# The first group's four x blocks begun together, feature by feature, and x fetched by two queues

## The chip, the cores and the metric

The kernel runs on one core of a Trainium2 chip. The metric is the device time in microseconds, 1324.78 as the median of three runs (1324.66 to 1325.58). One further execution was taken by the profiler; it took 1324.6 us, and its span, from the first to the last instruction, is 1322.9 us. TensorE (PE) multiplies, VectorE (DVE) and ScalarE (ACT) do the element-wise work, GpSimd (POOL) masks and starts transfers, SyncE (SP) starts the weight transfers.

## The reference

Two layers over 512 tokens of 1024 features: a Mamba-2 mixer and a ConvFFN, then differential attention and a second ConvFFN. Only the head of the Mamba-2 mixer is touched:

```python
zxbcdt = rms_norm(x, ln_g) @ in_w           # z 2048, x 2048, B 512, C 512, dt 32 columns
xbc = silu(causal_dwconv(xbc, conv_w, conv_b))
dt = softplus(dt + dt_bias); a = dt * (-exp(a_log))
y = ssd_chunked(xs * dt, a, B, C)           # 4 chunks of 128 tokens, 4 groups of 8 heads
y = (y + xs * d_skip) * silu(z)             # then a norm per group, and @ out_w
```

In `ssd_chunked` the running sums of `a` within a chunk give decays between tokens (a 128 x 128 matrix per head and chunk) and decays into and out of the chunk's state.

## The kernel before

**Products.** Every float32 product is made of three: an operand is split into a high part (ACT: `wh`, `xgh`) and the rest (DVE: `wl`, `xgl`), and `mm3` (L195) adds high by high, high by low and low by high. A block of the input projection is 128 output columns by 512 tokens in one PSUM bank: 8 features of 128 rows, 3 matmuls each, 24 in all (L196 to L198). The norm's factor per token, `rr`, is multiplied in when DVE takes the block out of PSUM.

**The start.** SP fetches x in four blocks of 128 tokens (`load_x`, L237): two, then the 32 dt columns (`dt_chunk`), then the first weight chunk (B of group 0, `in32`), then the other two. ACT's queue fetches the gain `st0` and the convolution's weights. TensorE runs seven placeholder products on the tile of ones (`busy`, L278), then turns each token block into features (`turn`, L287) in four auxiliary banks; a bank holds two features of two token blocks, that is of half the tokens. `split_x` (L292) takes a feature's half out as `xgh` and `xgl`, in the order `TURNS` = 0, 2, 4, 6, 1, 3, 5, 7. As the halves come, `dt_part` and `b0_part` (L298, L308) do dt and B's block in halves of 256 tokens, with small placeholder products between the first. The second half's `turn` needs the banks that the first half's splits release.

**Then** come, each as a whole block: C (`in36`), the four x blocks (`in16` to `in19`), and the first z block, `in0`. Weights come through `plan` in order of use: `chunk` (L187) asks for a chunk two ahead, SP fetches it into one of three raw buffers, ACT and DVE split it into one of three pairs. Each block goes to `conv_silu` (L610): DVE multiplies by `rr`, ACT starts the width-4 convolution, DVE adds three shifted terms, ACT applies SiLU.

**Decays.** dt is turned to tokens, softplus is a chain of some twenty small DVE operations (L645 to L664), then three matmuls `ps_dec` (L668) give the running sums, ACT their exponential, DVE copies, TensorE turns them (L687), and POOL writes them to DRAM (`cumd`) and reads them back spread over partitions (`fetch`, L706). POOL masks them and ACT takes 32 exponentials (`decays`). `scan` (L811) then goes through the four chunks, woven with the remaining z blocks.

**What sets the order.** A planner orders the instructions of each engine at compile time by priority, which follows the order of the program, and by its own estimate of when each is ready; on the chip each engine then goes through its list in that order. `pin` keeps an instruction in the program's order among the pinned ones of its engine; `tc.high_priority` moves a stretch ahead by an offset. Transfers are issued in order per queue.

Of the kernel before, what the change touches and what calls it, by code (L numbers as in the profile page):

```python
# [38 lines left out]
def trunk_kernel(ctx: ExitStack, tc, x, ssm_ln_g, ssm_in_w, ssm_conv_w, ssm_conv_b, ssm_dt_bias,  # L39
# [28 lines left out]
    plan.append(("dt", *w_cols(in_w, 0, KB, DI + CONV_DIM, NH)))  # L68

# [59 lines left out]
    WARM = (7, 64)  # L129
# [6 lines left out]
    def emit_chunk(pin=lambda i: i, later=None):  # L136
# [25 lines left out]
        else:  # L162
            def convert():
                pin(act.activation(wh[:, :n], raw[:, :n], AF.Copy))  # L164
                pin(dve.tensor_tensor(out=wl[:, :n], in0=raw[:, :n], in1=wh[:, :n].bitcast(F32), op=ALU.subtract))  # L165
# [7 lines left out]
    def dt_chunk():  # L173

        key, src, nk, ncol = plan[0]
        state["next"] = state["use"] = 1
        raw = wrp.tile([P, 1024], F32, tag="raw", name="wr_dt")
        rv = raw[:, :nk * ncol].rearrange("p (k c) -> p k c", k=nk)
        wv = w_dt.rearrange("p (k j c) -> p k j c", k=nk, j=2)
        sync.dma_start(rv, src)  # L180

        def convert():
            pin(act.activation(wv[:, :, 0, :], rv, AF.Copy))
            pin(dve.tensor_tensor(out=wv[:, :, 1, :], in0=rv, in1=wv[:, :, 0, :].bitcast(F32), op=ALU.subtract))
        return wv, convert
# [9 lines left out]
    def mm3(ps, wh, wl, xh, xl, start, stop):  # L195
        pe.matmul(ps, wh, xh, start=start, stop=False)  # L196
        pe.matmul(ps, wh, xl, start=False, stop=False)  # L197
        pe.matmul(ps, wl, xh, start=False, stop=stop)  # L198


# [30 lines left out]
    with tc.tile_pool(name="ph0", bufs=1) as p0:  # L231
# [4 lines left out]
        later = []  # L236
        load_x = lambda b: sync.dma_start(xt[b], x[0, b * P:(b + 1) * P, :])  # L237
# [60 lines left out]
        def dt_part(h, i):  # L298
            k, ts = TURNS[i], half[h]
            both = lambda: pin(pe.matmul(ps_dt[:2 * NH, ts], wdt[:, k].rearrange("p j c -> p (j c)"),  # L300
                                         xgh[k][:, ts], start=(i == 0), stop=(i == KB - 1)))
            if i < KB - 1:
                both()
            pin(pe.matmul(ps_dt[:NH, ts], wdt[:, k, 0, :], xgl[k][:, ts], start=False, stop=False))
            if i == KB - 1:
                both()

        def b0_part(h, i):  # L308
            k, ts = TURNS[i], half[h]
            pin(pe.matmul(ps_b0[:, ts], wb0[0][:, k, :], xgh[k][:, ts], start=i == 0, stop=False))  # L310
            pin(pe.matmul(ps_b0[:, ts], wb0[0][:, k, :], xgl[k][:, ts], start=False, stop=False))

        def b0_rest(h, i0=0, i1=KB):
            for i in range(i0, i1):
                k, ts = TURNS[i], half[h]
                pin(pe.matmul(ps_b0[:, ts], wb0[1][:, k, :], xgh[k][:, ts], start=False, stop=i == KB - 1))

        TURNS = (0, 2, 4, 6, 1, 3, 5, 7)
# [3 lines left out]
        ps_dt, ps_b0 = mm_bank("ps_dt"), mm_bank("ps_in32")  # L322
        wb0 = ready[0][1:]
        for b in range(2):
            for q in range(4):
                turn(0, b, q)
        for i in range(KB):
            if i == 1:
                convert_dt()
            split_x(0, TURNS[i])  # L330
        later.pop()()
        emit_chunk(pin, later)
        pv.append([view(aux_bank("xgt1_%d" % q)) for q in range(4)])
        for i in range(KB):
            dt_part(0, i)
            if i < 4:
                busy(1, WARM[1])
            elif i >= 6:
                turn(1, 2, i - 6)
        turn(1, 2, 2)  # L340
        turn(1, 2, 3)
        for i in range(KB):
            b0_part(0, i)
            if 1 <= i < 5:
                turn(1, 3, i - 1)
        b0_rest(0)
        for i in range(KB):
            split_x(1, TURNS[i])
        later.pop()()
        for i in range(KB):  # L350
            dt_part(1, i)
            b0_part(1, i)
        b0_rest(1)
        junk = [p0.tile([P, D], F32, name="sq%d" % i) for i in range(2)]
        for b in range(2):
            pin(act.activation(junk[0], xt[b], AF.Square, accum_out=rs[:, b:b + 1]))
            pin(dve.tensor_tensor_reduce(junk[1], xt[b + 2], xt[b + 2], 1.0, 0.0, ALU.mult, ALU.add,
                                         rs[:, b + 2:b + 3]))
        emit_chunk(pin)
        chunk("in32")  # L360
        ps = aux_bank("pst")
        pe.transpose(ps[:, :120], st1, ident[:120, :120])
        dve.tensor_copy(c1[:, :120], ps[:, :120])
# [22 lines left out]

    def rsqrt(v, pl, name, shape, n):

        m = pl.tile(shape, F32, tag="rs_m", name="rsm_" + name, bufs=2)
        t = pl.tile(shape, F32, tag="rs_t", name="rst_" + name, bufs=2)  # L390
        dve.tensor_scalar(out=m, in0=v, scalar1=1.0 / n, scalar2=EPS, op0=ALU.mult, op1=ALU.add)
        dve.tensor_scalar(out=v.bitcast(I32), in0=m.bitcast(I32), scalar1=1, scalar2=None,
                          op0=ALU.logical_shift_right)
        dve.tensor_scalar(out=v.bitcast(I32), in0=v.bitcast(I32), scalar1=-1, scalar2=0x5F3759DF,
                          op0=ALU.mult, op1=ALU.add)
        for _ in range(3):
            dve.tensor_tensor(out=t, in0=v, in1=v, op=ALU.mult)
            dve.scalar_tensor_tensor(out=t, in0=t, scalar=-0.5, in1=m, op0=ALU.mult, op1=ALU.mult)
            dve.scalar_tensor_tensor(out=v, in0=t, scalar=1.5, in1=v, op0=ALU.add, op1=ALU.mult)
# [26 lines left out]
    def along_tokens(r, name, step=2):  # L426

        ps = aux_bank("al_" + name)
        for b in range(NT):
            pe.transpose(ps[:, b * P:(b + 1) * P], r[:, step * b:step * b + 1].to_broadcast([P, P]), ident)  # L430
        return ps
# [984 lines left out]
```

## Time and profile before

| What | Value |
|---|---|
| Median of three runs | 1324.78 us (1324.66 to 1325.58) |
| Profiled execution | 1324.6 us |
| its span | 1322.9 us |
| TensorE busy | 1314.1 us, 99% |
| VectorE busy | 1026.0 us, 78% |
| ScalarE busy | 679.4 us, 51% |
| First whole block (C) begins | 20.94 us |
| First z block ends | 56.3 us |

An engine counts as busy while an instruction of its own runs; matmuls overlap each other, and their ends are modelled, so one matmul's length is read from the distance between starts. Lines such as L289 are those of the kernel. A row of the order of time has the start, the length, the engine (PEld is TensorE's weight load, SPq and ACTq are queues that start transfers), the line, the operation, its output and inputs, and in brackets the idle time just before it and what ended that. A count x8 means eight like instructions merged into one row.

### The profile page before, as it was taken

The page shows a single profiled execution, that of the slowest core. Times are in us where ns is not written, and L with a number is a line of the kernel's source. Part 1 is how long each engine was busy: PE and PEld are TensorE (multiplying, and loading weights), DVE is VectorE, ACT ScalarE, POOL GpSimd, SP SyncE. Part 2 cuts the span into 40 slices and gives each one's busy share as a digit, 9 for nine tenths or more (in the row PEclk, how much of TensorE's full clock was granted, in tenths as well). Part 3 has the DMA queues.
Part 4 walks back from the last instruction along what each step waited for, and adds up shares of the span by engine and source line. Part 5 has one row for each costly group of instructions (what it writes and reads, how often), then busy time and mean ns, then how long its engine had stood idle before and what let it go on. Part 6 is the DMA issues. An engine that isn't in the chain of part 4 may idle for free.

```text
span 1322.9 us, 17237 instructions
## 1 busy us (share of the span) xinstructions
PE 1314.1 (99%) x6441; PEld 1084.6 (82%) x6441; DVE 1026.0 (78%) x1740; ACT 679.4 (51%) x1148; POOL 59.4 (4%) x96
## 2 busy tenths in 40 slices
PE   9999999999999999999999999999999999999998
PEld 8778788888888888888888887777898888888887
DVE  6898977878868786878779645787778787778777
ACT  5665536336364443444345645776574443444343
POOL 5330300300000000000000000000000000000000
PEclk9999999999999999999999999999999999999999
DMA  7553432532317306320620333221236206320601
GB/s 208 156 152 96 152 97 79 167 96 66 109 50 239 96 0 206 105 73 1 205 82 1 117 103 88 71 80 57 64 95 209 80 1 222 96 65 0 213 27 64
DMA packets 166771, 135.09 MB, mean 102 GB/s; under 512 B 6044, under 2 KB 137824, under 8 KB 166688
## 3 DMA queue, kind: packets, MB, share of 16 engines
q1 hardware_dynamic: 161920, 121.75, 30.9%
q0 software_dynamic: 4496, 12.05, 3.0%
q8 instruction: 51, 0.84, 0.3%
q14 instruction: 32, 0.26, 0.1%
q10 hardware_dynamic: 272, 0.18, 0.0%
HBM read 131.72 MB, written 2.25 MB: 101 GB/s over the span
## 4 chain that ended last, share of the span: by engine, by line
PE 91%; DVE 5%; ACT 2%; DMA 1%; issue 1%; SPq 0%; DVEq 0%; ACTq 0%
PE ps_g L916 18%; PE ps_u L916 18%; PE ps_y L1061 7%; PE ps_x L1061 7%; PE ps_out L540 7%; PE ps_in L196 4%; PE ps_in L197 4%; PE ps_in L198 4%; PE ps_ao L540 3%; PE ps_k L1116 3%; PE ps_v L1116 3%; PE ps_q L1116 3%; PE ps_z L1061 2%; PE lg L1213 1%; PE po L1262 1%; DVE wl_in L165 1%
## 5 line engine op out<-in xcount | busy, mean ns | idle before, releaser
L916 PE MATMUL ps_g<-xgh,wl_g 128*128 128x512 f32 (+1 forms) x368 | 139.9, 380 | 0.0
L916 PE MATMUL ps_g<-xgl,wh_g 128*128 128x512 f32 (+1 forms) x368 | 139.9, 380 | 0.0
L916 PE MATMUL ps_g<-xgh,wh_g 128*128 128x512 f32 (+1 forms) x368 | 139.8, 380 | 0.0
L916 PE MATMUL ps_u<-xgh,wh_u 128*128 128x512 f32 (+1 forms) x368 | 139.3, 380 | 0.0
L916 PE MATMUL ps_u<-xgl,wh_u 128*128 128x512 f32 (+1 forms) x368 | 139.1, 380 | 0.0
L916 PE MATMUL ps_u<-xgh,wl_u 128*128 128x512 f32 (+1 forms) x368 | 137.6, 380 | 0.0
L196 PE MATMUL ps_in<-xgh,wh_in 128*128 128x512 f32 x312 | 125.5, 402 | 0.0
L197 PE MATMUL ps_in<-xgl,wh_in 128*128 128x512 f32 x312 | 123.8, 397 | 0.0
L198 PE MATMUL ps_in<-xgh,wl_in 128*128 128x512 f32 x312 | 122.3, 392 | 0.0
L989 ACT ACTIVATE wh_f<-dr 128x1024 fp32r<-128x1024 f32 (+1 forms) x72 | 71.3, 990 | 86.3 <-PE ps_y L1061 31.2
L990 DVE TENSOR_TENSOR wl_f<-dr,wh_f 128x1024 fp32r<-128x1024 f32 (+1 forms) x72 | 81.5, 1134 | 30.4 <-ACT wh_f L989 29.0
L165 DVE TENSOR_TENSOR wl_g<-wr_g,wh_g 128x1024 fp32r<-128x1024 f32 x44 | 53.8, 1224 | 51.9 <-ACT wh_g L164 51.9
L1006 ACT ACTIVATE hh<-f 128x256 fp32r<-128x256 f32 (+2 forms) x66 | 46.2, 700 | 77.6 <-DVE f L1018 74.2
L165 DVE TENSOR_TENSOR wl_u<-wr_u,wh_u 128x1024 fp32r<-128x1024 f32 x44 | 53.8, 1224 | 34.3 <-ACT wh_u L164 34.2
L916 PEld LDWEIGHTS ps_g<-xgh,wl_g 128*128 128x128 f32 x368 | 69.2, 188 | 13.4 <-DVE wl_g L165 0.2
L916 PEld LDWEIGHTS ps_g<-xgh,wh_g 128*128 128x128 f32 x368 | 69.2, 188 | 13.1
L916 PEld LDWEIGHTS ps_g<-xgl,wh_g 128*128 128x128 f32 x368 | 69.2, 188 | 13.1
L916 PEld LDWEIGHTS ps_u<-xgl,wh_u 128*128 128x128 f32 x368 | 69.2, 188 | 13.1
L916 PEld LDWEIGHTS ps_u<-xgh,wh_u 128*128 128x128 f32 x368 | 69.2, 188 | 13.1
L916 PEld LDWEIGHTS ps_u<-xgh,wl_u 128*128 128x128 f32 x368 | 68.2, 188 | 13.1
L1015 ACT ACTIVATE vg<-vg 128x512 f32<-128x512 f32 x44 | 27.9, 633 | 91.1 <-DVE vg L953 91.1
L953 DVE SCALAR_TENSOR_TENSOR vu<-ps_u,cf,vu 128x511 f32<-128x511 f32 x88 | 65.7, 747 | 9.6 <-ACT vu L951 8.6
(354 smaller groups left out, 3169.3 us busy)
## 6 DMA issues: line engine op xcount, KB each, us to landing
wr_g<-in_ffn_up_w_dram SPq DMA_DIRECT2D x44, 512.0 KB, 3.9
wr_u<-in_ffn_up_w_dram SPq DMA_DIRECT2D x44, 512.0 KB, 4.0
wr_in<-in_ssm_in_w_dram SPq DMA_DIRECT2D x40, 512.0 KB, 3.9
dr<-in_ffn_down_w_dram SPq DMA_DIRECT2D x16, 1024.0 KB, 9.4
m<-cumd POOLq DMA_DIRECT2D x16, 512.0 KB, 5.2
wr_out<-in_ssm_out_w_dram SPq DMA_DIRECT2D x16, 512.0 KB, 4.0
dr<-in_ffn_down_w_dram SPq DMA_DIRECT2D x8, 768.0 KB, 8.3
wr_k<-in_kv_w_dram SPq DMA_DIRECT2D x8, 512.0 KB, 3.8
```

Source lines behind the costliest of these rows:

```text
L165: pin(dve.tensor_tensor(out=wl[:, :n], in0=raw[:, :n], in1=wh[:, :n].bitcast(F32), op=ALU.subtract))
L196: pe.matmul(ps, wh, xh, start=start, stop=False)
L197: pe.matmul(ps, wh, xl, start=False, stop=False)
L198: pe.matmul(ps, wl, xh, start=False, stop=stop)
L540: m = pe.matmul(ps, x, w[:, k % 2, :], start=k == 0 and i == 0, stop=k == 3 and i == 2)
L916: pin(pe.matmul(ps[:, ts], a[:, k, :], x[k][:, ts], start=k == 0 and i == 0, stop=k == KB - 1 and i == 2))
L953: dve.scalar_tensor_tensor(out=v[:, s:], in0=ps[:, :T - s], scalar=col(2 - s), in1=v[:, s:], op0=ALU.mult, op1=ALU.add)
L989: act.activation(wh, src, AF.Copy)
L990: dve.tensor_tensor(out=wl, in0=src, in1=wh.bitcast(F32), op=ALU.subtract)
L1006: act.activation(fl(h[:, lo:hi, :]), fl(f[:, lo:hi, :]), AF.Copy)
L1061: pin(pe.matmul(bank[b], x, w_[:, q - a, :], start=start and q == 0 and i == 0, stop=end and q == a + n - 1 and i == 2, skip_group_check=T ...
L1116: m = pe.matmul(pss[b], x[k][:, ts], a[:, k - k0, :], start=k == 0 and i == 0, stop=k == KB - 1 and i == 2)
```

## The change

- **Transfers.** Blocks 0 and 1 are fetched in halves of 64 partitions, one by SP and one by ACT (`load_halves`). The x blocks' weights are fetched by feature instead of by block: one slice (`load_w`) has 128 rows of 512 columns, all four blocks' columns for one feature, into buffers of their own (`rawx`). SP's order is: half of block 0, slice 0, half of block 1, slice 1, block 2, slice 2, block 3, slices 3 to 7, dt's columns (`raw_dt`), then `plan`, which starts with B and C and has no dt and no x of group 0. The gain `st0` goes second in ACT's queue.
- **Start.** Instead of dt and B the halves feed the four x blocks, in the four main PSUM banks: `x_part(i, ts)` does feature `TURNS[i]` for all four blocks, 12 matmuls. Features 0 to 3 of the order go by halves, the fifth at full width for all blocks (`BY_BLOCK`), the last three block by block (`x_rest`). `split_w` splits a slice, and the splits of slices 0, 1 and 2 stand ahead of the features' splits. dt follows at full width in an auxiliary bank. One placeholder product stands in place of four.
- **Order behind it.** The root of the norm and the dt chain come earlier in the program, the chain at high priority. Then x0 to x3, B, C and the first z block, pinned; the decays' matmuls after C, and their transposes behind the first four features (12 matmuls) of the first z block (`turn_decays`). `fetch`, `params_a` and `turn_b` of group 0 come after that z block.

```diff
-    plan.append(("dt", *w_cols(in_w, 0, KB, DI + CONV_DIM, NH)))
...
-        for b in range(4):
-            plan.append(in_chunk(16 + 4 * g + b))
+        if g:
+            for b in range(4):
+                plan.append(in_chunk(16 + 4 * g + b))
...
-    WARM = (7, 64)
+    WARM = (7, 1)
+
+    BY_HALF, BY_BLOCK = 4, 5
...
-        load_x = lambda b: sync.dma_start(xt[b], x[0, b * P:(b + 1) * P, :])
-        load_x(0)
-        load_x(1)
-        wdt, convert_dt = dt_chunk()
-        emit_chunk(pin, later)
+        rawx = [p0.tile([P, 1024], F32, name="rawx%d" % i) for i in range(KB // 2)]
+        raw_dt = p0.tile([P, KB, NH], F32, name="raw_dt")
+        load_x = lambda b: pin(sync.dma_start(xt[b], x[0, b * P:(b + 1) * P, :]))
+        cols_of = lambda i: slice((i % 2) * 512, (i % 2 + 1) * 512)
+        load_w = lambda i: pin(sync.dma_start(rawx[i // 2][:, cols_of(i)],
+                                              in_w[TURNS[i] * P:(TURNS[i] + 1) * P, DI:DI + 512]))
+
+        def load_halves(b):
+
+            for q, ps in ((sync, slice(0, 64)), (act, slice(64, P))):
+                pin(q.dma_start(xt[b][ps], x[0, b * P + ps.start:b * P + ps.stop, :]))
+
+        load_halves(0)
+        pin(act.dma_start(st0, ssm_ln_g.rearrange("o (b p) -> (o b) p", p=P)))
+        load_w(0)
+        load_halves(1)
+        load_w(1)
         load_x(2)
+        load_w(2)
         load_x(3)
-        act.dma_start(st0, ssm_ln_g.rearrange("o (b p) -> (o b) p", p=P))
+        for i in range(3, KB):
+            load_w(i)
+        pin(sync.dma_start(raw_dt, in_w[:, DI + CONV_DIM:DI + CONV_DIM + NH].rearrange("(k p) c -> p k c", p=P)))
...
+        def split_w(i):
+            (h, l), r, cs = wx[i // 2], rawx[i // 2], cols_of(i)
+            pin(act.activation(h[:, cs], r[:, cs], AF.Copy))
+            pin(dve.tensor_tensor(out=l[:, cs], in0=r[:, cs], in1=h[:, cs].bitcast(F32), op=ALU.subtract))
+
+        def x_part(i, ts, blocks=range(4)):
+            (h, l), k = wx[i // 2], TURNS[i]
+            for j, (w, f) in enumerate(((h, xgh), (l, xgh), (h, xgl))):
+                for b in blocks:
+                    c = (i % 2) * 512 + b * P
+                    pin(pe.matmul(ps_x[b][:, ts], w[:, c:c + P], f[k][:, ts],
+                                  start=i == 0 and j == 0 and ts.start == 0, stop=i == KB - 1 and j == 2,
+                                  skip_group_check=True))
...
+        busy(WARM[1], 64)
+        for i in range(3):
+            side(i)
         for i in range(KB):
-            if i == 1:
-                convert_dt()
+            if i < 3:
+                split_w(i)
             split_x(0, TURNS[i])
-        later.pop()()
-        emit_chunk(pin, later)
+        split_w(3)
...
+        for i in range(3):
+            x_part(i, half[0])
+        for qs in ((0, 1), (2, 3)):
+            for b in (2, 3):
+                for q in qs:
+                    turn(1, b, q)
+            if qs[0] == 0:
+                x_part(3, half[0])
         for i in range(KB):
             split_x(1, TURNS[i])
-        later.pop()()
-        for i in range(KB):
-            dt_part(1, i)
-            b0_part(1, i)
-        b0_rest(1)
+            if i in (4, 6):
+                split_w(2 + i // 2)
...
+        for i in range(4):
+            x_part(i, half[1])
...
+        for i in range(BY_HALF, BY_BLOCK):
+            x_part(i, slice(0, T))
         emit_chunk(pin)
...
+        x_rest(0)
...
+                if g == 0:
+                    if b:
+                        x_rest(b)
+                    conv_silu(b, ps_x[b], xs[b])
+                    continue
...
+            if g == 0:
+                conv_block(16, "in32", bT, True)
+                conv_block(20, "in36", cT, True)
...
+                z = z_blocks(g, zs, (4, turn_decays))
+                next(z)
+                for c in cs:
+                    c.fetch()
+                params_a()
+                turn_b(g, bT, cs)
```

More of the change, by code (lines that the diff above doesn't have):

```diff
@@ L134, in trunk_kernel, with emit_chunk @@
     pin = tc.keep_in_program_order
[L136 removed]
+    def emit_chunk(pin=lambda i: i):
         i = state["next"]
@@ L296, in split_x, with side @@
                                          in1=xgh[m][:, half[h]].bitcast(F32), op0=ALU.mult, op1=ALU.subtract))
[L298 to L318, printed above, removed]
+        def side(i):
+            wx.append([wp.tile([P, 1024], F32R, tag=t, name="%s_x%d" % (t, i)) for t in ("wh", "wl")])
+        def split_w(i):
[10 more added lines that the diff above has]
+                                  skip_group_check=True))
         half = (slice(0, 256), slice(256, T))
@@ L321, in trunk_kernel @@
         pv = [[view(aux_bank("xgt0_%d" % q)) for q in range(4)]]
[L322 to L326, printed above, removed]
+        ps_x = [mm_bank("ps_in%d" % (16 + b)) for b in range(4)]
+        wx = []
+        for q in range(4):
+            turn(0, 0, q)
+        for q in range(4):
+            turn(0, 1, q)
+        busy(WARM[1], 64)
+        for i in range(3):
+            side(i)
@@ L358, in trunk_kernel @@
                                          rs[:, b + 2:b + 3]))
-        emit_chunk(pin)
[L360 to L363, printed above, removed]
+        for i in range(4):
+            x_part(i, half[1])
+        ps = aux_bank("pst")
+        pin(pe.transpose(ps[:, :120], st1, ident[:120, :120]))
+        pin(dve.tensor_copy(c1[:, :120], ps[:, :120]))
+        rsqrt(rs, bp, "x", [P, NT], D)
@@ new lines, in trunk_kernel @@
+        side(3)
+        split_w(6)
+        split_w(7)
+        ps_dt = aux_bank("ps_dt")
+        for k in range(KB):
+            both = lambda: pin(pe.matmul(ps_dt[:2 * NH], wv[:, k].rearrange("p j c -> p (j c)"), xgh[k],
+                                         start=k == 0, stop=k == KB - 1))
+            if k < KB - 1:
+                both()
+            pin(pe.matmul(ps_dt[:NH], wv[:, k, 0, :], xgl[k], start=False, stop=False))
+            if k == KB - 1:
+                both()
+        for i in range(BY_HALF, BY_BLOCK):
+            x_part(i, slice(0, T))
@@ L365, in params_a, with x_rest @@
+        emit_chunk(pin)
+        def x_rest(b):
+            for i in range(BY_BLOCK, KB):
+                x_part(i, slice(0, T), (b,))
+        x_rest(0)
+        dtT = bp.tile([P, T], F32, tag="xn1", name="dtT")[:2 * NH, :]
+        pin(act.activation(dtT, ps_dt[:2 * NH, :], AF.Copy))
     def params_a():
@@ L596, in trunk_kernel, with in_block, conv_block @@
     with tc.tile_pool(name="ssm_y", bufs=1) as yp, tc.tile_pool(name="ssm", bufs=1) as sp:
-        def in_part(ps, wh, wl, ts):
-            for k in range(KB):
-                mm3(ps[:, ts], wh[:, k, :], wl[:, k, :], xgh[k][:, ts], xgl[k][:, ts], k == 0, k == KB - 1)
-        def in_block(key):
+        def in_block(key, fixed=False, between=None):
             wh, wl = chunk(key)
             ps = mm_bank("ps_" + key)
-            in_part(ps, wh, wl, slice(0, T))
-            return ps
-        def conv_block(j, key, dst):
-            conv_silu(j, in_block(key), dst)
+            for k in range(KB):
+                if between and k == between[0]:
+                    between[1]()
+                mm3(ps, wh[:, k, :], wl[:, k, :], xgh[k], xgl[k], k == 0, k == KB - 1, pin if fixed else lambda i: i)
+            return ps
+        def conv_block(j, key, dst, fixed=False):
+            conv_silu(j, in_block(key, fixed), dst)
         def conv_silu(j, ps, dst):
@@ L667, in trunk_kernel @@
-        ps = aux_bank("ps_dec")
-        pe.matmul(ps[:, 0:P], lt, A, start=True, stop=True)
-        pe.matmul(ps[:, P:2 * P], ut, A, start=True, stop=True)
-        pe.matmul(ps[:, 2 * P:3 * P], ones, A, start=True, stop=True)
-        dec = sp.tile([P, 3 * P], F32, name="dec")
-        act.activation(dec, ps[:, :3 * P], AF.Exp)
-        dl, et = dec[:, 0:P], dec[:, 2 * P:3 * P]
-        split = lambda a: a.rearrange("p (i b j) -> p i j b", b=4, j=2)
-        rows = lambda a: a.rearrange("p (i j b) -> p i j b", j=2, b=4)
@@ L685, in trunk_kernel @@
         cumd = [dp.tile([NT * NG, HPG * P], F32, name="cumd%d" % i) for i in range(2)]
-        for i in range(2):
-            pe.transpose(ps[:, i * P:(i + 1) * P], cum[:, i, :], ident)
-            dve.tensor_copy(cumT[:, i, :], ps[:, i * P:(i + 1) * P])
-            pool.dma_start(cumd[i].rearrange("i (q t) -> (i q) t", t=P), cumT[:, i, :])
         fl = lambda a: a.rearrange("p a b -> p (a b)")
@@ L875, in trunk_kernel @@
             for c in cs:
                 c.decays()
-            z = z_blocks(g, zs)
-            next(z)
+            if g:
+                z = z_blocks(g, zs)
+                next(z)
             weave(scan(cs), z, 2, 3)
```

182 lines of the change are left out of this document (82 added, 100 removed).

## The prediction

> **What bounds it now.** I read the page's busy times and its chain of waits first, then the span cut into stretches at the points where the kernel's stages meet, then the first 21 us instruction by instruction.
>
> ```profile
> PE 1314.1 (99%) x6441; PEld 1084.6 (82%) x6441; DVE 1026.0 (78%) x1740; ACT 679.4 (51%) x1148; POOL 59.4 (4%) x96
> ...
> PE 91%; DVE 5%; ACT 2%; DMA 1%; issue 1%; SPq 0%; DVEq 0%; ACTq 0%
> ```
>
> ```profile
> 0.00:8.49 8.49, 6.68 (x31) 5.99 (x31) 1.69 (x7) 2.66 (x5) 2.83 (x10) 1.00 0.84 203
> 8.49:11.26 2.77, 2.66 (x22) 2.22 (x23) 2.69 (x7) 2.77 (x7) 0.00 (x0) 1.00 0.95 372
> 11.26:20.92 9.66, 9.63 (x83) 9.58 (x84) 7.93 (x13) 7.71 (x16) 6.03 (x13) 1.00 0.77 194
> 20.92:56.16 35.24, 35.24 (x167) 29.08 (x166) 32.33 (x74) 20.22 (x28) 13.10 (x26) 1.00 0.49 139
> 56.16:86.60 30.44, 29.68 (x190) 22.85 (x189) 25.62 (x42) 17.69 (x42) 11.39 (x15) 1.00 0.68 186
> 86.60:200.00 113.40, 112.40 (x567) 92.27 (x567) 97.53 (x159) 59.27 (x100) 14.39 (x20) 1.00 0.42 121
> ```
>
> The columns after the stretch are its length and the busy us of PE, PEld, DVE, ACT and POOL, then granted clock, DMA share and GB/s. TensorE sets the end: from 20.92 us on it never stops for long. Idle after that are 0.76 us between 56 and 87 us and 1.00 us up to 200 us. So a change at the start is worth what it does to TensorE's lost time before 20.9 us, plus whatever stall it makes or removes behind that. Busy time does not show what is lost, because placeholder matmuls on the tile of ones and slow first transposes count as busy. The order of time does:
>
> ```profile
> 0.81 0.87 SPq L237 DMA_DIRECT2D xt<-in_x_dram  x2
> 1.13 3.35 PE L280 MATMUL warm<-ones 128*128 128x128 f32 x14 [1.13 <-DVE ones L202]
> 4.63 1.57 PEld L289 LDWEIGHTS xgt<-ident,xt 128*128 128x128 f32 x8
> 6.38 1.19 PEld L289 LDWEIGHTS xgt<-ident,xt 128*128 128x128 f32 x8 [0.18 <-DMA xt<-in_x_dram]
> 7.11 0.48 ACT L294 ACTIVATE xgh<-xgt,g 128x256 fp32r<-128x256 f32 x1 [4.40 <-PE xgt L289]
> 8.49 0.33 PE L300 MATMUL ps_dt<-xgh,w_dt 128*64 128x256 f32 x1 [0.68 <-DVE w_dt L184]
> 11.65 0.69 PEld L289 LDWEIGHTS xgt<-ident,xt 128*128 128x128 f32 x6
> 19.96 1.12 PE L316 MATMUL ps_in<-xgh,wl_in 128*128 128x256 f32 x8
> 20.94 0.48 PE L196 MATMUL ps_in<-xgh,wh_in 128*128 128x512 f32 x1
> ```
>
> A transpose costs 0.69 / 6 = 0.115 us once TensorE runs at full rate, a half-width (256 column) matmul about (1.12 - 0.28) / 7 = 0.12 us, 0.28 being the last one's own length. Before 20.94 us the kernel has done 32 transposes (3.7 us), 32 dt halves and 48 B halves (80 x 0.12 = 9.6 us): 13.3 us of useful work in 20.9 us, so **7.6 us lost**. 4.6 us of this is the wait for the first token block.
>
> **The change, part by part.** Bytes first. In the new order the queues carry block 0 (0.52 MB), the first weight slice (0.26), block 1, slice 1, block 2, slice 2, block 3, slices 3 to 7, the dt columns, then B's chunk.
>
> ```profile
> 2.83 8.32 DMA xt<-in_x_dram
> ...
> 12.55 0.18 POOL L253 COPY landed<-xt 128x1 f32<-128x1 f32 x1 [8.50 <-DMA xt<-in_x_dram]
> ```
>
> ```profile
> 3.50:4.00 0.50, 0.50 (x4) 0.50 (x4) 0.00 (x0) 0.00 (x0) 0.50 (x2) 1.00 1.09 418
> ...
> 7.00:7.50 0.50, 0.50 (x6) 0.50 (x5) 0.00 (x0) 0.39 (x2) 0.00 (x0) 1.00 1.21 204
> 7.50:8.00 0.50, 0.31 (x3) 0.07 (x1) 0.38 (x1) 0.50 (x3) 0.00 (x0) 1.00 1.34 166
> ```
>
> With x alone in flight the DMA engines are full at 418 GB/s (share 1.09), so fetching a block by two queues can't move its bytes faster; it saves an issue of 0.87 / 2 = 0.44 us at best, and I take 0. The slice ahead of block 1 costs 0.26 MB / 0.4 = 0.65 us, so block 1 lies ready at 6.38 + 0.65 = 7.0 us instead of 6.38 (bounds 6.4, if ACT's half overtakes the slice, and 7.8, if the slump to 166 to 204 GB/s catches it). Before, block 2 landed at 2.83 + 8.32 = 11.15 us and block 3 by 12.55 us behind 0.66 MB of dt and B weights in short rows. Now slice 2 ends 2.36 MB of long rows. From block 1 at 6.36 us (1.05 MB) 1.31 MB more take 3.3 us at 0.4 MB/us, 9.6 us; with the slump (about 0.8 us) 10.4. I take 10.2, bounds 9.6 and 11.2 (block 2's present landing); block 3 follows 1.3 us later, slice 3 another 0.65 us.
>
> Then the splits. ACT and DVE now do, in a fixed order, slice 0, feature 0, slice 1, feature 2, slice 2, the other six features, slice 3.
>
> ```profile
> 7.79 2.66 ACT L294 ACTIVATE xgh<-xgt,g 128x256 fp32r<-128x256 f32 x7
> 8.36 2.83 DVE L295 SCALAR_TENSOR_TENSOR xgl<-xgt,g,xgh 128x256 fp32r<-128x256 f32 x7
> ...
> 27.43 0.58 ACT L632 ACTIVATE rr<-al_x 128x512 f32<-128x512 f32 x1
> 29.07 0.68 DVE L612 TENSOR_TENSOR u<-ps_in,rr 128x512 f32<-128x512 f32 x1
> ```
>
> A feature costs 2.66 / 7 = 0.38 on ACT and 0.40 on DVE; a 128x512 slice has no row, and the nearest of that shape are 0.58 on ACT and 0.68 on DVE. ACT's first feature starts 7.11 - 6.38 = 0.73 us behind block 1's transposes: 7.75, done at 8.25. TensorE's first x part (12 halves, 1.44 us) runs 8.25 to 9.7; the second, with slice 1 there by 8.5 and its feature at 9.4, to 11.1. Slice 2 at 10.2 is split at 10.8, its feature at 11.2: the third part runs 11.2 to 12.65. Everything queued behind slice 2 on ACT (six features) is late with it: the second half's transposes need the first half's banks, freed by the features at 12.75 and 13.15, so the next eight end at 13.85; slice 3's low part is done at 14.6, part 3 at 15.55, eight more transposes at 16.5, and four parts of the second half (5.8 us) at 22.3. By then useful work is 32 transposes and 96 halves, 3.7 + 11.5 = 15.2 us: **7.1 us lost against 7.6, a gain of 0.5**. Bounds: block 1 at 6.4 makes it 1.1; slice 2 at 11.2 makes it -0.5. The fillers that go (three of four small ones) were never on the path, since they stood in gaps. The dt matmuls at full width stand against more x halves (96 halves for 80), under 0.1 us.
>
> The rest is order. After 22.3 us come dt (16 x 0.23), one whole x part (12) and block 0's remainder (9), 37 full matmuls:
>
> ```profile
> 21.73 0.39 PE L196 MATMUL ps_in<-xgh,wh_in 128*128 128x512 f32 x1
> ...
> 22.42 0.39 PE L196 MATMUL ps_in<-xgh,wh_in 128*128 128x512 f32 x1
> ...
> 26.50 0.60 PE L430 MATMUL al_x<-ident,rs 128*128 128x128 f32 x4
> ...
> 27.42 0.50 PE L196 MATMUL ps_in<-xgh,wh_in 128*128 128x512 f32 x1
> ```
>
> Three take 0.69, one 0.23, so 8.5 us: 30.8. The transposes that spread the norm's factor and turn dt take 27.42 - 26.50 = 0.9 and are now fixed at this place: 31.7. DVE's splits of the last slices, its squares and the root of x lie under these. The decays' transposes are now fixed behind the first 12 matmuls (2.76 us) of the first z block, and TensorE's queue stands still if they are not ready; the rest of z and every later matmul are queued behind them.
>
> ```profile
> 45.00 0.39 PE L670 MATMUL ps_dec<-A,ones 128*128 128x128 f32 x2
> 46.23 0.49 ACT L672 ACTIVATE dec<-ps_dec 128x384 f32<-128x384 f32 x1
> 47.50 0.23 DVE L682 COPY cum<-dec 128x128 f32<-128x128 f32 x1
> ...
> 60.49 1.10 PE L759 MATMUL st<-xe,bt 128*128 128x512 f32 x2 [0.76 <-DVE xe L746]
> ```
>
> Before, from the end of ps_dec (45.39) to the last copy (47.73) passed 2.34 us, under 2.76: cost 0, upper bound 1.2 (one weight split of DVE more, below). In exchange x's convolutions come first, so the states' operand xe should no longer be late: 0 to 0.76 us gained, I take 0.3, the nearer to 0 as DVE is no less loaded. Sum: 0.5 + 0.3 = 0.8 us. The profiled execution took 1324.6 us (span 1322.9 and 1.7 around it), so 1323.8; the median of the runs, 1324.78, is 0.2 higher: **1324.0 us**. What a measurement of this kernel tells from no change is about 0.2%, 2.65 us; the forecast lies inside. Its own range is 1322.9 (1.1 and 0.76 us gained) to 1326.5 (0.5 and 1.2 us lost).
>
> **Rivals.** *DVE becomes the bound (slower).*
>
> ```profile
> 27.52 0.29 DVE L645 COPY dt<-ps_dtt 128x128 f32<-128x128 f32 x1 [1.54 <-PE ps_dtt L637]
> 53.49 2.32 DVE L617 SCALAR_TENSOR_TENSOR ctmp<-u,c,ctmp 128x511 f32<-128x511 f32 x3
> 55.93 0.40 PE L198 MATMUL ps_in<-xgh,wl_in 128*128 128x512 f32 x1
> ...
> L165 DVE TENSOR_TENSOR wl_in<-wr_in,wh_in 128x1024 fp32r<-128x1024 f32 x5 | 6.1, 1222 | 0.3 <-ACT wh_in L164 0.3
> ```
>
> The norm's factor comes to DVE behind those 37 matmuls: dt's copies, 1.0 us behind the first of the spreading transposes (27.52 - 26.50), start at 31.8 us, 4.3 later. DVE then had work without a gap to 55.8 us, 28.3 us, of which one weight split of 1.2 us now lies earlier. It ends its convolutions at 31.8 + 27.1 = 58.9, while TensorE, with 27 matmuls of x, 48 of B and C and 24 of z left (99 x 0.23) and about 0.9 us of decays, is through the first z block at 55.4 (before: 56.3). If the next z block, whose weights DVE must split in the same queue, doesn't cover that, TensorE waits 3.5 us: 1324.8 - 0.5 + 3.5 = 1327.8 us. It decides once DVE's lag exceeds the z matmuls that are ready, 5.5 us a block. For it: DVE's 32.33 of 35.24 busy, and the present 0.76 us wait of just this kind. Against: those z matmuls need only one split.
>
> *More than the start (faster).* Block 1 at 6.4 (1.1 us gained), the 0.76 us gone, and the 1.00 us of idle time up to 200 us gone too, for the scan of the first group runs with less behind it: 2.9 us, 1321.9. Against: those stalls lie in later groups, whose order isn't touched, and no row ties them to the first.
>
> *TensorE stays slow longer.* The first eight transposes took 1.57 / 8 = 0.196 us each, later ones 0.115, with a granted clock of 1.00 in every stretch shown: it is 1.7 times slower until about 7 us. Now TensorE stands from 6.2 to 7.0 us. If the slow rate lasts to the end of the second part, 24 halves cost 0.085 us more each, 2.0 us: 1326.0. The Trainium skill, page "TensorE: Matmul & The Clock Gate", Part 1, has the clock halved until a free-running window of about 3.4 us has been busy, and Part 4 says transposes don't count as busy in the same way; by it a window that misses would cost up to 1.7 us, an estimate. The trace agrees on the slow start, but its granted clock doesn't show it. Against: 0.68 us of standing at 7.8 us did no harm before.
>
> **How the numbers follow.** Forecast 0.66, DVE 0.15, faster 0.11, slow TensorE 0.08. The DVE case lies mostly beyond 2.65 us over 1324.78 with a tail inside (0.12 and 0.03), slow TensorE mostly inside (0.05, and 0.03 beyond). Slower 0.15, faster 0.11, within 0.2% 0.74. The range reaches from the faster case, 1321.9, to near the DVE case, 1327.2.
>
> **What would show it.** Right: the second block's transposes at about 7.0 us, the first x part at about 8.2, no wait of more than 0.3 us before the third part, the first full-width dt matmul near 22.3, the decays' transposes without a wait, 0.76 us at the states gone or smaller. Wrong: ACT standing for slice 2 past 11 us; TensorE standing after the first z block; transposes still at 0.2 us each beyond 7.1 us; a first x part before 7.6 us, for then the two queues did bring x sooner.

## The result, and the profile after

The changed kernel takes **1332.6 us** (median of six runs, 1332.24 to 1333.38) against 1324.55 for the kernel before on the same chip: a ratio of 1.0058, with a 95% interval of 1.0047 to 1.0068. By that ratio it is 7.7 us slower (by the two medians 8.05; the losses below go by the ratios); the forecast was 1324.0. The profiled execution took 1333.0 us with a span of 1331.3, 8.4 us more than before.

The same stretches of the span as before (length, busy us of PE, PEld, DVE, ACT and POOL, granted clock, DMA share, GB/s), for the changed kernel:

```profile
0.00:8.49 8.49, 4.47 (x23) 4.04 (x23) 1.52 (x5) 1.91 (x2) 2.25 (x8) 0.94 0.75 157
8.49:11.26 2.77, 0.00 (x0) 0.00 (x0) 0.00 (x0) 0.00 (x0) 0.00 (x0) 0.50 1.01 258
11.26:20.92 9.66, 9.09 (x55) 9.12 (x56) 5.22 (x11) 4.78 (x12) 4.13 (x9) 0.66 1.12 334
20.92:56.16 35.24, 35.24 (x197) 29.45 (x196) 28.66 (x69) 20.00 (x34) 10.85 (x21) 1.00 0.25 63
56.16:86.60 30.44, 28.06 (x147) 21.32 (x145) 26.48 (x41) 24.68 (x52) 11.29 (x17) 1.00 0.65 184
86.60:200.00 113.40, 111.90 (x607) 91.84 (x607) 100.10 (x161) 56.65 (x97) 21.50 (x27) 1.00 0.44 130
```

In the second row no compute engine does anything for 2.77 us, while the DMA engines are busy all the time (share 1.01) and yet move 258 GB/s, where the kernel before had 372. From there to 20.92 us the granted clock is 0.66 on average. In the fifth row TensorE is idle for 2.38 us where it was 0.76, in the sixth for 1.50 where it was 1.00. TensorE in order of time shows both places:

```profile
5.89 0.20 PE L296 MATMUL pst<-ident,st 8*128 8x8 f32 x1 [1.52 <-DMA st<-in_ssm_ln_g_dram]
6.06 1.06 PE L301 MATMUL xgt<-ident,xt 128*128 128x128 f32 x8
11.83 1.94 PE L301 MATMUL xgt<-ident,xt 128*128 128x128 f32 x8 [4.71 <-DMA xt<-in_x_dram]
13.85 1.20 PE L324 MATMUL ps_in<-xgh,wh_x 128*128 128x256 f32 x4
...
28.91 0.27 PE L369 MATMUL pst<-ident,st 120*128 120x120 f32 x1
...
60.14 0.27 PE L890 MATMUL ps_cum<-ident,cum 128*128 128x128 f32 x1
...
77.08 1.16 PE L745 MATMUL yo<-cT,S 128*128 128x128 f32 x8 [2.38 <-DVE xd L734]
```

Block 1 of x reaches TensorE at 11.83 us instead of 6.38, after a wait of 4.71 us. The halves of the x blocks end at 28.91 us (the next row is the first thing behind them); 15.2 us of useful work stand before that point, so 13.7 us are lost there instead of 7.6: **6.1 us** of the 8.4. The later wait for xd adds 1.6, and the stretch up to 200 us 0.5.

The second place on DVE (two rows) and on GpSimd (one row):

```profile
71.83 3.98 DVE L167 TENSOR_TENSOR wl_in<-wr_in,wh_in 128x1024 fp32r<-128x1024 f32 x1
...
76.34 0.68 DVE L734 TENSOR_TENSOR xd<-xs,dt 128x512 f32<-128x512 f32 x1
```

```profile
71.55 3.19 POOL L711 TENSOR_SCALAR_AFFINE_SELECT m<-m 128x1024 f32<-128x1024 f32 x3
```

A weight split, 1.22 us on average in the page's rows of the later weights, took 3.98 us, just while GpSimd did three masks in a row, and xd is queued behind it.

### The profile page after: what moved, and what is told of

Read it like the earlier page. It is cut to its first block, busy times and chain, and to the rows that moved or that the text cites. A ratio compares the mean times of both kernels' runs of the same rounds, so it can differ in the third digit from the quotient of the medians.

```text
span 1331.3 us, 17269 instructions
## 1 busy us (share of the span) xinstructions
PE 1314.5 (99%) x6443; PEld 1085.8 (82%) x6443; DVE 1027.3 (77%) x1744; ACT 679.1 (51%) x1152; POOL 62.5 (5%) x96
## 4 chain that ended last, share of the span: by engine, by line
PE 95%; DVE 3%; ACT 1%; DMA 1%; issue 0%; SPq 0%; DVEq 0%
PE ps_g L942 18%; PE ps_u L942 18%; PE ps_y L1087 7%; PE ps_x L1087 7%; PE ps_out L557 7%; PE ps_in L180 5%; PE ps_in L181 5%; PE ps_in L182 5%; PE ps_k L1142 3%; PE ps_ao L557 3%; PE ps_v L1142 3%; PE ps_q L1142 3%; PE ps_z L1087 2%; PE ps_in L324 2%; PE lg L1239 1%; PE po L1288 1%
## 5 line engine op out<-in xcount | busy, mean ns | idle before, releaser
L180 PE MATMUL ps_in<-xgh,wh_in 128*128 128x512 f32 x288 | 115.4, 401 | 0.0
L181 PE MATMUL ps_in<-xgl,wh_in 128*128 128x512 f32 x288 | 114.8, 399 | 0.0
L182 PE MATMUL ps_in<-xgh,wl_in 128*128 128x512 f32 x288 | 112.9, 392 | 0.0
```

The source lines that it names most:

```text
L180: pin(pe.matmul(ps, wh, xh, start=start, stop=False))
L181: pin(pe.matmul(ps, wh, xl, start=False, stop=False))
L182: pin(pe.matmul(ps, wl, xh, start=False, stop=stop))
```

## The experiments

My theory after these rows: (1) a transfer of 64 neighbouring partitions moves at about half the rate, (2) the long stop it makes also halves the clock, (3) apart from both, the new order lets three masks meet a weight split. All three are guesses at this point. The rivals: the second queue, the longer byte order, and a DVE that is full. Each time below is a median with its ratio to the kernel before, timed on the same chip in the same job (1325.65, 1324.74, 1324.37 and 1325.75 us in the four jobs: a1 to a4, b1 to b4, c1 and c2, d1 and d2).

### Whole blocks, columns, one queue

```diff
# a1_whole
-        load_halves(0)
+        load_x(0)
...
-        load_halves(1)
+        load_x(1)
# a2_columns
-            for q, ps in ((sync, slice(0, 64)), (act, slice(64, P))):
-                pin(q.dma_start(xt[b][ps], x[0, b * P + ps.start:b * P + ps.stop, :]))
+            for q, cs in ((sync, slice(0, 512)), (act, slice(512, D))):
+                pin(q.dma_start(xt[b][:, cs], x[0, b * P:(b + 1) * P, cs]))
# a3_one_queue
-            for q, ps in ((sync, slice(0, 64)), (act, slice(64, P))):
+            for q, ps in ((sync, slice(0, 64)), (sync, slice(64, P))):
```

> The changed kernel, but blocks 0 and 1 of x fetched whole by SP, in the same place of the same byte order; every engine's order is otherwise that of the changed kernel. Theory 1 (a transfer into 64 partitions runs at half the rate, so the halves stretch the whole start): block 1's transposes begin at 7.0 to 7.8 us instead of 11.8, the last half-width x matmul ends at 22 to 24 us instead of 28.9, the time is 1325.5 to 1327.5 us against 1332.6, and what is left above the kernel before is the 2 us of TensorE waits between 56 and 200 us. Theory 2 (the weight slices ahead of block 1 and more bytes in all keep block 1 back): block 1 stays beyond 10 us and the time above 1330. Theory 3 (two queues disturb each other): as theory 1.

> The changed kernel, but each half of blocks 0 and 1 is 512 columns of all 128 partitions instead of all columns of 64 partitions; SP still takes one and ACT the other. Theory 1 (64 partitions): block 1 at 7.0 to 7.8 us, time 1325.5 to 1327.5 us, within 1 us of the kernel with whole blocks. Theory 3 (two queues): block 1 stays at 10 to 12 us, 1331 to 1333 us. Theory 2 (bytes in front): as theory 3.

> The changed kernel, but both halves of 64 partitions are issued by SP, one after the other; no second queue. Theory 1 (64 partitions): block 1 at 10 to 13 us and 1331 to 1334 us, packets of the halves at about 300 ns. Theory 3 (two queues): block 1 at 7 to 8 us, 1325.5 to 1327.5 us.

Block 1's transposes on TensorE, in a1_whole, a2_columns and a3_one_queue in turn:

```profile
7.43 1.97 PE L301 MATMUL xgt<-ident,xt 128*128 128x128 f32 x8 [0.85 <-DMA xt<-in_x_dram]
```

```profile
9.15 1.97 PE L301 MATMUL xgt<-ident,xt 128*128 128x128 f32 x8 [1.98 <-DMA xt<-in_x_dram]
```

```profile
11.13 1.94 PE L301 MATMUL xgt<-ident,xt 128*128 128x128 f32 x8 [3.40 <-DMA xt<-in_x_dram]
```

| Kernel | Time, us | Ratio to before | x halves end |
|---|---|---|---|
| a1_whole | 1329.16 | 1.0030 (1.0018 to 1.0041) | 23.30 |
| a2_columns | 1329.63 | 1.0035 (1.0021 to 1.0049) | 25.09 |
| a3_one_queue | 1331.82 | 1.0054 (1.0037 to 1.0070) | 27.95 |

With every engine's order as in the changed kernel, the form of the first two blocks' transfers alone moves block 1 by up to 4.4 us. That is one execution each; in b2_small_masks and b4_late_decays below, which fetch x as a1_whole does, block 1's transposes begin at 8.38 and 7.08 us, so about 1 us of such a difference can be chance. Halves of 64 partitions are slow on one queue too (11.13 us), so the second queue isn't what makes them so. Halves by columns, all 128 partitions each, cost 0.5 us of time by the ratios, less than the noise; their block 1 came 1.35 us later than I expected. Nothing arrives earlier by two queues: 9.15 against 7.43 us. But a1_whole is still 4.0 us slower than before, 1.7 us above the range I expected, though its start is within 1 us of my sum (23.30 against 22.3): there is a second cause.

### The even and the odd partitions

```diff
-            for q, ps in ((sync, slice(0, 64)), (act, slice(64, P))):
-                pin(q.dma_start(xt[b][ps], x[0, b * P + ps.start:b * P + ps.stop, :]))
+            for q, odd in ((sync, 0), (act, 1)):
+                pin(q.dma_start(xt[b][odd::2], x[0, b * P + odd:(b + 1) * P:2, :]))
```

> The changed kernel with the same two transfers per block on the same two queues, but the even partitions by SyncE's queue and the odd ones by ScalarE's, instead of partitions 0 to 63 and 64 to 127; each transfer still has 64 rows of 4 KB. Theory (what is slow is the range of neighbouring partitions, not the number of rows): block 1's transposes at about the 9.2 us of a2_columns or before, between 7.5 and 9.7, TensorE's wait there under 2.6 us; time within 1.5 us of a2_columns, some 4 to 5 us over the kernel before. Rival (64 rows a transfer are slow, wherever they lie): block 1 at 11 to 12.5 us, time 7 to 8 us over the kernel before.

The transfers' totals between 3 and 5 us: d2_after_rows_first (below; its x comes in neighbouring halves, on the same chip), d1_even_odd, and a1_whole with whole blocks. Behind them stand block 1's transposes in d1_even_odd:

```profile
DMA packets 227, 0.51 MB, mean 253 GB/s; under 512 B 52, under 2 KB 70, under 8 KB 227
```

```profile
DMA packets 310, 0.69 MB, mean 343 GB/s; under 512 B 67, under 2 KB 86, under 8 KB 310
```

```profile
DMA packets 405, 0.74 MB, mean 369 GB/s; under 512 B 68, under 2 KB 176, under 8 KB 405
```

```profile
9.89 1.97 PE L301 MATMUL xgt<-ident,xt 128*128 128x128 f32 x8 [2.10 <-DMA xt<-in_x_dram]
```

The median of the first 128 packets of 4 KB (as many as the two halves of one queue have), from the trace's records of single packets, on SyncE's queue and on ScalarE's:

```
changed kernel        288 ns   170 ns
d2_after_rows_first   200 ns   212 ns
b1_before_halves      269 ns   273 ns
d1_even_odd           159 ns   159 ns
a1_whole              159 ns   -
```

As many rows of 4 KB in as many transfers run at 159 ns a packet, as in whole blocks, if they go to every second partition: the rate is a matter of which partitions, not of how many rows, and the rival falls. It was not simply half, as I had put it: packets of neighbouring halves took 1.1 to 1.8 times as long, and not equally on the two queues (a3_one_queue: 236 ns, where I expected about 300). The 2 KB packets of the weight slices show it as well: those that started in the first 10 us took 84 ns (median) in d1_even_odd and a1_whole, and 153 in the changed kernel, whose slices share the DMA engines with the halves. The Trainium skill, page "SBUF — State Buffer", section "Door 1: The DMA port swizzle", says that 64 neighbouring partitions reach only half of the ports, and its section "Can I just issue two DMAs to hit both halves?" answers no; the packets agree with the first in kind, and the even partitions show that the range decides.

The time is 1331.5 us, 1.0036 (1.0025 to 1.0048), by the ratio about that of a2_columns as expected (by the medians 5.75 us over the kernel before). Block 1 came 0.2 us later than the expected bound, at 9.89 us: between 6 and 7.5 us the DMA engines moved little there (53 to 127 GB/s). The other kernels have such a slump at about that time too (39 to 223 GB/s between 6 and 8 us in a1_whole); its cause stays open, and so does what it adds to block 1 in each run. Block 1's arrival alone would not have decided: in d2_after_rows_first, with neighbouring halves, it came only 0.4 us later, at 10.31 us. The packets decide; the time fits, 1.0036 against 1.0058 for the changed kernel, with intervals that just touch.

### Halves alone in the kernel before

```diff
-        load_x(0)
-        load_x(1)
+        for b in range(2):
+            for q, ps in ((sync, slice(0, 64)), (act, slice(64, P))):
+                q.dma_start(xt[b][ps], x[0, b * P + ps.start:b * P + ps.stop, :])
```

> The kernel before, with nothing of the new order in it: only blocks 0 and 1 of x come in halves of 64 partitions, the upper half by SyncE's queue, the lower by ScalarE's. Theory (a transfer of 64 partitions moves at about half the rate, whatever is beside it): 1.05 MB at the 150 to 170 GB/s of the changed kernel's start, so that block 1's transposes begin at 9 to 10 us and not before 7, TensorE stands more than 2 us before them, and the time is 3 to 6 us longer than before. Rival (halves are slow only where two-KB rows of the weight slices run between them): block 1 within 0.7 us of before, time within 1 us of before.

```profile
8.96 0.24 PE L285 MATMUL pst<-ident,st 8*128 8x8 f32 x1 [4.47 <-DMA st<-in_ssm_ln_g_dram]
9.13 3.28 PE L290 MATMUL xgt<-ident,xt 128*128 128x128 f32 x16
```

1328.91 us, 1.0032 (1.0020 to 1.0043): **4.2 us lost by this part of the change alone**, with no slice between. In the rows, of TensorE, the small gain transfer, queued behind both halves on ScalarE's queue, comes last and holds TensorE at 8.96 us. Block 0 landed at 6.19 us and the last half of block 1 at 8.77, where block 1 fetched whole had landed at 6.34. Behind the stop the granted clock was 0.50 from 8.5 to 11.3 us. How the 4.2 us divide among the halves, the gain's place in the queue and the clock, this run doesn't show.

### The stop filled

```diff
         for q in range(4):
             turn(0, 0, q)
+        busy(18, P)
         for q in range(4):
             turn(0, 1, q)
```

> The changed kernel with 18 placeholder products between the transposes of block 0 and those of block 1, 4.2 us at full rate, in the time in which TensorE waits for block 1. Nothing else differs in any engine's order. If the halved clock of the profiled execution (0.50 from 8.5 to 11.3 us, 0.66 from 11.3 to 20.9) costs what the slow transposes and first x parts show, about 2.5 us, the time falls to 1330.1; if it costs little, because the splits and not TensorE set the pace there, it stays within 1 us of 1332.6. If the clock is the main cause of the loss, below 1328.

```profile
7.51 5.01 PE L292 MATMUL warm<-ones 128*128 128x128 f32 x36
12.36 1.04 PE L301 MATMUL xgt<-ident,xt 128*128 128x128 f32 x8
13.24 0.33 PE L292 MATMUL warm<-ones 128*128 128x64 f32 x2
13.38 0.72 PE L324 MATMUL ps_in<-xgh,wh_x 128*128 128x256 f32 x4
```

With placeholder products through the stop, block 1's eight transposes take 1.04 us and not 1.94, four half-width matmuls 0.72 and not 1.20. From those transposes to the end of the halves pass 14.36 us (12.36 to 26.72) against 17.08 (11.83 to 28.91): the slow clock costs **2.7 us** in the changed kernel's profile. That is one execution. Over the six, the mean granted clock went from 0.996 to 1.000 and the time by only 1.1 us, but that mean leaves out the first microseconds (last section), so the clock's share in the median stays open. The time is 1331.34 us, 1.0053 (1.0032 to 1.0074); the fillers ran past block 1's arrival, so the whole gain isn't seen, and against the changed kernel's 1.0058 the timing alone doesn't settle it.

### The masks

```diff
-                pool.affine_select(out=self.m, in_=self.m, pattern=[[0, HPG], [1, P]],
+                n = HPG if self.g else 1
+                pool.affine_select(out=self.m[:, :n, :], in_=self.m[:, :n, :], pattern=[[0, n], [1, P]],
...
-                    pin(act.activation(v, v, AF.Exp, bias=ncum[:, col:col + 1]))
+                    pin(act.activation(v, v, AF.Exp, bias=(ncum if self.g else ut)[:, col:col + 1],
+                                       scale=1.0 if self.g else 0.0))
```

> a1_whole with 7/8 of the first group's masks left out (GpSimd masks one head of eight of each chunk) and its decay values replaced by constants of the same shape (ScalarE's exponentials still run on every head, on scale 0). Theory (DVE's split of a weight chunk is stopped by GpSimd's masks beside it, and xd, queued behind it, keeps TensorE from the carried states' product): the split at its usual 1.2 us and not 3.5, the 2.77 us wait at that product gone to under 0.5, no halved clock after it, time 2 to 4 us below a1_whole, 1324.5 to 1327. Rival (the new order itself brings xd late, DVE being full): the wait stays above 2 us and the time within 1 us of a1_whole's 1329.2.

DVE, GpSimd and TensorE in a1_whole (one row each), then a1_whole's stretch behind the wait with its columns as above, then DVE and GpSimd in b2_small_masks:

```profile
66.30 3.50 DVE L167 TENSOR_TENSOR wl_in<-wr_in,wh_in 128x1024 fp32r<-128x1024 f32 x1
...
66.56 4.19 POOL L711 TENSOR_SCALAR_AFFINE_SELECT m<-m 128x1024 f32<-128x1024 f32 x3
...
71.95 2.07 PE L745 MATMUL yo<-cT,S 128*128 128x128 f32 x8 [2.77 <-DVE xd L734]
```

```profile
72.00:75.80 3.80, 3.80 (x13) 3.33 (x14) 1.31 (x2) 3.80 (x14) 1.09 (x1) 0.55 0.98 232
```

```profile
67.33 1.36 DVE L167 TENSOR_TENSOR wl_in<-wr_in,wh_in 128x1024 fp32r<-128x1024 f32 x1
68.61 0.68 DVE L758 TENSOR_TENSOR S<-S,dec 128x512 f32<-128x512 f32 x1
...
67.04 0.56 POOL L712 TENSOR_SCALAR_AFFINE_SELECT m<-m 128x128 f32<-128x128 f32 x2
```

With short masks the split takes 1.36 us, TensorE has no idle time from 24 to 90 us, its clock stays at 1.00 there, and the time is 1324.37 us, 0.9999 (0.9990 to 1.0008): that of the kernel before. So what a1_whole loses, 4.0 us, hangs on the masks, within the noise of some 2 us: 2.77 us of waiting, and behind it a clock of 0.55 for 3.8 us, some 1.7 us more (3.8 x 0.45, an estimate). DVE being full is not the cause. This kernel leaves out most of the masks' work and one input of the exponentials as well as the meeting; c1_rows_first below leaves out nothing and only moves the masks.

```diff
-                z = z_blocks(g, zs, (4, turn_decays))
+                z = z_blocks(g, zs, (7, turn_decays))
```

> a1_whole with the decays turned behind seven of the first z block's eight steps instead of four, so 9 matmuls, about 2.1 us, later; everything of the masks follows by as much. Theory (the meeting of GpSimd's masks and DVE's split is a matter of their times): masks start near 68.6 us, after the split of 66.3, which takes 1.2 to 2 us; the wait at the carried states' product falls from 2.77 to under 1.2 us; time 1 to 3 us below a1_whole, unless a later step (the masked products waiting for the exponentials) stands in its place. Rival (DVE's load brings xd late): the wait stays within 0.7 us of 2.77 and the time of a1_whole's.

TensorE and GpSimd in b4_late_decays:

```profile
55.96 0.27 PE L890 MATMUL ps_cum<-ident,cum 128*128 128x128 f32 x1
...
59.55 1.07 POOL L701 DMA_DIRECT2D m<-cumd  x2 [1.27 <-DMA cumd<-cumT]
...
66.10 4.19 POOL L711 TENSOR_SCALAR_AFFINE_SELECT m<-m 128x1024 f32<-128x1024 f32 x3
```

This run didn't move what it was to move: the transposes came 1.4 us later than in a1_whole (54.53), but the fetch of m and the masks no later than there (59.59 and 66.56), for GpSimd waits at both for transfers. The split still met the masks, and TensorE's wait stayed at 2.50 us. The time, 1327.08 us, 1.0019 (1.0008 to 1.0029), overlaps a1_whole's interval. It tells nothing of the masks' time.

### The byte order, and then the masks apart

```diff
# b3_blocks_first, on a1_whole
-        load_w(0)
         load_x(1)
+        load_w(0)
         load_w(1)
# c1_rows_first, on b3_blocks_first (fetch split in its two parts)
-                for c in cs:
-                    c.fetch()
+                cs[0].fetch("m")
+                for c in cs:
+                    c.fetch("e")
+                for c in cs[1:]:
+                    c.fetch("m")
```

> a1_whole with the two first token blocks ahead of the first weight slice in SyncE's queue (block 0, block 1, slice 0, slice 1, block 2 and so on). Theory (the bytes ahead of block 1 set the 0.85 us wait at 7.43 us): block 1's transposes at 6.5 to 6.9 us, the wait under 0.3; the first x part at 9.2 to 9.5, for the splits still stand behind the copies of the transposes, if slice 0 is there by 7.5 us; time 0 to 0.7 us below a1_whole. Rival (slice 0 then comes late): first x part after 9.6, time the same or longer.

```profile
4.62 2.56 PE L301 MATMUL xgt<-ident,xt 128*128 128x128 f32 x16
7.63 0.74 PE L324 MATMUL ps_in<-xgh,wh_x 128*128 128x256 f32 x4 [0.28 <-ACT xgh L306]
...
10.04 0.74 PE L324 MATMUL ps_in<-xgh,wh_x 128*128 128x256 f32 x4 [0.72 <-ACT xgh L306]
```

No wait is left between the two blocks, the first x part starts at 7.63 us, 1.6 earlier than I expected, and the clock is full from there. The slices then come late for the next parts, and the halves end at 22.99 us, only 0.3 earlier than in a1_whole. 1328.29 us, 1.0020 (1.0009 to 1.0030); the masks still meet the split.

> b3_blocks_first with the first group's fetches in another order in GpSimd's queue: chunk 0's decay table (m), then the six er pieces of all chunks, then m of chunks 1 to 3; before, m0, m1, er, er, m2 and so on. Nothing else moves in any engine's order. Theory (three masks in a row stop DVE's split): m0 is there early and is masked when the issues are through, at about 65.9 us, m1 to m3 land later and no two masks stand back to back over the split of 65.9 us; the split takes 1.2 to 2.4 us and not 3.24, the wait at the carried states' product falls from 2.53 to under 1.5 us and the halved clock behind it goes; time 1 to 3.5 us below b3_blocks_first, 1321.5 to 1325.5, about the kernel before. Rival (the masks only shift together): wait over 2 us, time of b3_blocks_first.

GpSimd, DVE and TensorE in c1_rows_first:

```profile
64.89 1.11 POOL L712 TENSOR_SCALAR_AFFINE_SELECT m<-m 128x1024 f32<-128x1024 f32 x1
71.68 1.09 POOL L712 TENSOR_SCALAR_AFFINE_SELECT m<-m 128x1024 f32<-128x1024 f32 x1 [5.68 <-DMA m<-cumd]
...
64.78 2.38 DVE L738 TENSOR_TENSOR xe<-xd,dec 128x512 f32<-128x512 f32 x2
67.68 1.21 DVE L167 TENSOR_TENSOR wl_in<-wr_in,wh_in 128x1024 fp32r<-128x1024 f32 x1
...
66.70 1.10 PE L751 MATMUL st<-xe,bt 128*128 128x512 f32 x2 [0.95 <-DVE xe L738]
```

> As c1_rows_first, but the er pieces stand ahead of all four m. Theory: the first m lands after 66.5 us, the split of 65.9 runs free in 1.2 us, the masks meet later and shorter work of DVE (S, xd, xe, each 0.68 us); the wait at the carried states' product under 1.2 us, time 1.5 to 4 us below b3_blocks_first unless the masked products then wait for the exponentials; if so, TensorE stands at y or at an xs transposition behind 70 us by about as long as m0 is later, 1 to 3 us, and the gain is gone. Rival: wait over 2 us, time of b3_blocks_first.

GpSimd's list came out the same for c1_rows_first and c2_two_then_two (the planner puts the er pieces, which wait for the second turned table, behind the first m in both), so the second is a repeat: 1325.44 us, 1.0006 (0.9997 to 1.0015), and 1325.37, 1.0008 (0.9999 to 1.0017). The masks stand apart, the split takes 1.21 us, one mask meets xe instead (2.38 us for two that take 1.28), and TensorE waits 0.95 us, as the kernel before did with 0.76. The new order without its two faults is as fast as the old; neither run beats it.

> The changed kernel, halves and all, with the fetch order of c1_rows_first as its only edit. Theory (the two losses are separate and add up): block 1 still at 11 to 12 us, no split over 2.5 us behind 60 us, the wait at the carried states' product under 1.2 us; 3 to 4.5 us below the changed kernel, that is 3.2 to 4.7 us over the kernel before. Rival (what is won there is lost elsewhere, since the late start hides it): within 1.5 us of the changed kernel, 6 us or more over the kernel before.

The same edit of the fetches on the changed kernel itself:

```profile
10.31 1.97 PE L301 MATMUL xgt<-ident,xt 128*128 128x128 f32 x8 [1.31 <-DMA xt<-in_x_dram]
...
70.29 1.10 PE L751 MATMUL st<-xe,bt 128*128 128x512 f32 x2 [1.10 <-DVE xe L738]
...
71.27 1.21 DVE L167 TENSOR_TENSOR wl_in<-wr_in,wh_in 128x1024 fp32r<-128x1024 f32 x1
```

1328.71 us, 1.0024 (1.0015 to 1.0033): 3.2 us over the kernel before instead of 7.7, with the halves as they were. Block 1 came at 10.31 us, earlier than the 11 to 12 I expected of the unchanged halves. Within the noise the two losses add up: the halves are worth 3.7 us (changed kernel less a1_whole), 4.2 (b1_before_halves) or 3.2 (d2_after_rows_first), the meeting of masks and split 4.1 (a1_whole less b2_small_masks), 4.5 (changed kernel less d2_after_rows_first) or, with a wait of 0.95 us left over, 1.9 (b3_blocks_first less c1_rows_first). Those that compare two jobs carry the uncertainty of both, about 2 us.

## Why the prediction was wrong

**Transfers: the step that failed.** "Fetching a block by two queues can't move its bytes faster ... and I take 0." That it isn't faster was right (9.15 us by columns, 7.43 whole); 0 was not its lower bound. I asked whether two queues add bandwidth and not what a transfer of half the partitions does to it. Block 1 came at 11.83 us, beyond the 7.8 I had as the bound; the price is 3 to 4 us of time. The runs showed in its place that halves of 64 neighbouring partitions take up to 1.8 times as long a packet (288 ns for 159) and hold the weight slices up too.

**TensorE stays slow longer** was a rival at 0.08 and 2.0 us; in the changed kernel it held with 2.7 us, on top of the late block. My reason against it, a standing of 0.68 us without harm, said nothing of one of 4.7 us. Nor was it right that the granted clock doesn't show the slow start: the column reads 1.00 there because the trace's clock records begin only at 7.11 us (last section). The start adds up: 28.91 - 22.3 = 6.6 us, of which 4.8 are block 1 (11.83 for 7.0), 2.7 the clock, and -0.9, the rest, waits for slices and splits that I had counted and that the late block hid (a4_filler, at full clock, takes 14.36 us from block 1's transposes to that point, where my sum had 22.3 - 7.0 = 15.3).

**The start without halves** was sized well: a1_whole's halves end at 23.30 us for 22.3, block 1 comes at 7.43 for 7.0. The gain I hoped for there, 0.5 us, was not had (8.1 us lost against 7.6): the first x part came at 9.48 us, not 8.25, behind block 1 and transposes of 0.25 us each.

**Decays at 0** was right: the fixed transposes stand at 60.14 us without a wait.

**The states' wait** was to shrink by 0.3 us of 0.76; in its place came 2.38, for xd and one product later. I saw that DVE would be late there and looked for its own load (the rival at 1327.8, with the convolutions ending at 58.9 us). The place was right and the mechanism wrong: DVE isn't full but stopped, by masks of an engine that I had read as 4% busy. The row of before that told of it was quoted, 0.76 us for xe, and I didn't ask why xe was late. DVE and GpSimd just ahead of that wait, in the kernel before:

```profile
58.76 1.58 DVE L746 TENSOR_TENSOR xe<-xd,dec 128x512 f32<-128x512 f32 x1
```

```profile
58.61 2.69 POOL L720 TENSOR_SCALAR_AFFINE_SELECT m<-m 128x1024 f32<-128x1024 f32 x2
```

An xe takes 0.68 us (the median of the kernel's twelve); this one took 1.58 beside two masks: the same meeting, with a shorter DVE operation.

Together: the start 6.6 us worse than predicted, the states' wait 1.9 (2.38 for 0.46), the stretch up to 200 us 0.5. That is 9.0 of the 9.2 us between the 1323.8 predicted for the profiled execution and its 1333.0.

## What to carry to other kernels

Before splitting a transfer over two queues, ask which partitions each half covers; cut by columns or leave it whole, and put ahead of it in the queue only what is needed sooner. When a reorder shifts a stage by a few us, list what runs beside each long two-input DVE operation there, also on an engine that is hardly busy: a GpSimd mask beside it can cost DVE about the mask's whole length (two xe 1.10 us longer beside one mask of 1.11 in c1_rows_first). A TensorE stop of some 2.5 us may bring a slow stretch behind it, which the price of the stop has to hold.

## What the runs showed of the hardware that was not expected

- **DVE and GpSimd stop each other.** A split of 1.22 us took 3.98 beside three masks, and the three masks 4.19 us in a1_whole where three take 3.19 in the changed kernel. The Trainium skill, page "SBUF — State Buffer", section "Who interferes with whom", says that a VectorE instruction with two SBUF inputs contends with a GpSimd one that reads SBUF; these rows agree.
- **Neighbouring halves are slow, and slow others.** 4 KB packets took 170 to 288 ns in the changed kernel and 159 with every second partition or whole blocks; 2 KB packets of weight slices that started in the first 10 us took 153 ns beside neighbouring halves and 84 without.
- **The granted clock.** Of the eight kernels that stopped before the carried states' product, five ran on at half clock for some 3.4 us (stops of 2.47 to 2.77 us), three did not (2.38, 2.70 and 2.70), so the length alone doesn't decide.
- **At the start the clock column reads 1.00 where nothing is recorded.** The trace's first clock record, of 1.00, stands at 7.11 us in the kernel before, at 10.53 in a1_whole and at 15.49 in d2_after_rows_first, and up to there TensorE is slow: in d2_after_rows_first four half-width matmuls take 1.05 us at 14.21 and 0.64 from 15.73 on. In the changed kernel the clock rose at 4.11 us, fell to 0.50 at 7.52, early in the long stop, and rose again at 17.76. The first rise differs by execution: b4_late_decays has the start of a1_whole and rose at 6.47. So the late block is not the only cause of a slow start, and one profile's price of it, the 2.7 us above too, holds for that execution.
